# A hybrid attention block on one core: the variance of x enters the norms ahead of the power, three more warming products, the last gate's second part later, the last scaling behind the last squares

## The chip, the core and the metric

The kernel runs on one core of one Trainium2 chip. A core has five engines that work side by side: TensorE (PE, matrix products), VectorE (DVE), ScalarE (ACT), GpSimd (POOL) and SyncE (SP, which here only starts transfers). Transfers between the chip's memory (HBM) and the core's SBUF run on 16 DMA engines. The metric is the device time of one execution in microseconds (us); lower is better.

## The reference

One transformer block on x of 512 tokens by 1024 features, all in float32. Cut to what matters:

```python
n = rmsnorm(h, g_mix)
(gq, gk, gv, gr, z_gf, z_gb, cq, ckv, kr, z_ma, z_mb) = split(n @ w_in)
y_gla = gla_branch(...)      # 4 heads: gated linear attention, both directions, chunks of 64
    # o = rmsnorm(o_f + o_b, g_gla) per head (256 wide); o * silu(gr)
y_mla = mla_branch(...)      # 8 heads: softmax attention
    # q = rmsnorm(cq, g_q) @ w_uq, kv = rmsnorm(ckv, g_kv) @ w_ukv, rope on 32 columns
h = h + (sigmoid(z_ma) * y_gla + sigmoid(z_mb) * y_mla) @ w_out
m = rmsnorm(h, g_mlp)
h = h + square(relu(m @ w_ff1)) @ w_ff2      # 4096 hidden
return rmsnorm(h, g_final)

def rmsnorm(x, g): return x * rsqrt(mean(x * x) + EPS) * g
```

## The kernel before

Features or tokens lie on the 128 partitions; a tile is mostly 128 x 512. Every float32 product is split into a high and a low part and done as three products in the format fp32r (high by high, low by high, high by low), so each operand has tiles with names ending in h and l. The large products (gv, gr, za, w_out and the MLP) use seven block products in place of eight.

The names that matter here:

- `x` is not normalised before it is projected. The products run on x times `g_mix` (tiles `xT`), and the norm's factor r_x = 1/sqrt(var + EPS), one value for each token, is multiplied in later. Each later norm of something that came from x must therefore allow for r_x. For the heads' norm, `gla_squares` (L1140) lets ACT square the output `gla<h>o`, DVE forms mean + EPS in the tile `gla<h>ss` (128 x 4), POOL raises it to the power −0.5 (`mhalf` is −0.5), and DVE multiplies by `r_x`. `gla_gated` (L1150) then multiplies it into the gates `gra`, `grb`, `grc`, `grd` (tiles of `g1`), and `gla_turn` (L1157) turns those on PE (tiles `y`). For the ranks `cq` and `ckv` of the second branch, `rstd_diag` (L618) does the same: mean times r_x squared (`r_x2`), plus EPS, the power on POOL, times `r_x`.
- The head of the program (L663 on) starts with 8 products of a tile of ones (`warm`), which nothing reads, and goes on with the first projections (`first`), whose weights `vw` and input `x` come by DMA. The input is scaled by a column of `gvec`, which is a transfer of its own.
- `zb0` to `zb7` are the eight feature tiles of the gate z_mb; `gated` scales and squashes each. For the last one (L1626 to L1629) three of the eight blocks of the sum over features run first (`range(3)`), `rotary_q` comes between, and then the other five (`range(3, KD)`).
- `up_units(0)` brings up the first pair of softmax heads (tiles `uq`, `uk`, `uv`, weights `wq0`, `wk0`; `wq1` belongs to the next pair). `lin.out()` is the output of the last linear head, `gla3o`, from scores `sc` and states `st`. `s` are the softmax scores.
- The final norm works by blocks of 128 tokens: squares of the two halves with a running sum (`out_squares`, `out_square`, ACT), mean (DVE) and power (POOL) in `hp`, then the left half is scaled on DVE (`out_left`, tiles `sy`, `sz`) and the right half on ACT (`out_right`, tiles `row`), and each half is stored.

What sets the order: from `nc.keep()` on, after the head, each operation is only recorded as a `Work`, and `nc.flush` lets the class `Due` put all of them in order. `Due` gives each operation a due time, counted back from the PE product that needs it, and then plays the program through with the durations of `Work.cost`. At each step an engine takes, among the operations that are ready, the one that is due first. DVE and POOL share one port in this model, and where both could begin, an operation that `yields` gives way. The engines then follow that order. So an altered cost, or an operation more or less, can move any operation behind the head. All operations are issued from one line of `lay` (L229), which is why every row of the profile has that line: the rows are told apart by their tiles' names.

Of the kernel before, what the change touches and what calls it, by code (L numbers as in the profile page):

```python
# [15 lines left out]
ALU = mybir.AluOpType  # L16
# [125 lines left out]
class Work:  # L142
    def __init__(self, engine, name, args, named):
        self.engine, self.name, self.args, self.named = engine, name, args, named
        self.is_dma = name == "dma_start"
# [12 lines left out]
        self.yields = name in ("tensor_copy", "tensor_scalar")  # L158
        self.func = args[2] if name == "activation" else None

    def cost(self):
# [8 lines left out]
        if self.engine == "scalar":  # L170
            table = self.func not in (None, AF.Copy, AF.Identity, AF.Square)
            more = (0.03 if table else 0) + (0.1 if "accum_out" in self.named and n > 256 else 0)
            return more + (0.217 + 0.000543 * n if self.from_psum else 0.09 + 0.000857 * n)
        if self.engine == "vector":
            if "scan" in self.name:
                return 0.32
            if self.name == "copy_predicated":
                return 0.2
            if self.name == "scalar_tensor_tensor":
                return 0.125 + 0.00105 * n if not self.psum else 0.17 + 0.00085 * n  # L180
            return 0.065 + (0.00105 if two or self.psum or self.name == "tensor_reduce" else 0.00066) * n
# [16 lines left out]
class Script:  # L198
# [19 lines left out]
    def told(self, work):  # L218
        if self.kept is not None:
            self.kept.append(work)  # L220
            return None
        return self.lay(work)
# [23 lines left out]
class Due:  # L246


    def __init__(self, todo, slots, head=0.0, tables=None):
# [16 lines left out]
        for i, w in enumerate(todo):  # L266
# [26 lines left out]
            after[i].discard(i)  # L293

# [92 lines left out]
def tile_block(ctx: ExitStack, tc: tile.TileContext, t, out: bass.AP):  # L387
# [216 lines left out]
    r_x, r_x2 = one([P, NT], F32, "r_x"), one([P, NT], F32, "r_x2")  # L604
# [59 lines left out]
    for _ in range(8):  # L664
        nc.tensor.matmul(warm[:, :P], ones, ones, start=True, stop=True)
# [44 lines left out]
    nc.vector.tensor_tensor(r_x2, r_x, r_x, op=ALU.mult)  # L710
# [429 lines left out]
    def gla_squares(h, os):  # L1140
# [488 lines left out]
    gated(proj_run(zb, xT, None, range(3, KD)), "b7")  # L1629
# [4 lines left out]
    for _ in units:  # L1634
        pass
    rs = gla_squares(h, os)
# [113 lines left out]
    def out_square(i, cols):  # L1750
        p = hparts[i]
        nc.scalar.activation(out_at[i][0][:, cols], hrow[i][:, cols], AF.Square, accum_out=p[:, 1:2])
# [17 lines left out]
    def out_right(i):  # L1770
        right, rs = out_at[i][1], hparts[i][:, 3:4]
        nc.scalar.activation(right, right, AF.Copy, scale=rs)
# [101 lines left out]
    class Plan:  # L1874
        def add(self, engine, cost, fn, reads=(), writes=(), lands=None):
            if fn:
                fn()
# [5 lines left out]
    def act(size, fn, reads, writes):  # L1883
        plan.add("ACT", COST["ACT"][size], fn, reads, writes)
# [291 lines left out]
    class Group:  # L2176


        def __init__(self, qd):
            self.qd, self.last = qd, qd == NQ - 1  # L2180
            self.corner, self.right, self.out_key = {}, {}, {}
# [128 lines left out]
        def last_half(self, x, bank):  # L2310
# [15 lines left out]
            act(QUART, lambda: out_square(3, cols), (("row", 3, 0, "h"),), (("hp", 3), self.out_key[3][0]))  # L2326
# [3 lines left out]
        def ended(self, i, squared=False):  # L2330
# [6 lines left out]
            act(HALFT, lambda: out_right(i), (hp, right), (right,))  # L2337
# [121 lines left out]
```

## Time and profile before

| | |
|---|---|
| time, median of 3 runs | 744.87 us (744.81 to 746.26) |
| time of the profiled execution | 744.94 us |
| its span, from first to last record | 743.2 us |
| granted TensorE clock, mean over the span | 0.997 |
| HBM read, written | 116.81 MB, 2.10 MB |
| POOL busy | 193.9 us (26%) |

The span leaves out what lies around the records. A row of the profile names the line, the engine, the operation, and the tiles as output<-inputs, with shapes as partitions x elements; "x4" counts instructions. In a timeline the first number is the start in us and the second the duration, and brackets at the end give the idle time before and the instruction that ended it. Matmuls are pipelined, so the duration of one row reaches into the next; the pace is read from start to start. A small product of plain float32 shows as two records. The clock of a window is given as a share of full speed.

### The profile page before, as it was taken

To read this page: it belongs to the slowest core of one execution; us is meant where nothing else is said; L and a number is where in the kernel's file an instruction comes from. 1 tells how busy PE (TensorE), PEld (TensorE's weight loads), DVE (VectorE), ACT (ScalarE), POOL (GpSimd) and SP (SyncE) were. 2 spreads that over 40 slices of the span, in tenths; PEclk is the share of its full clock that TensorE was granted. 3 is DMA by queue.
4 is the path that set the end of the run, shared out by engine and by line. 5 is a ranking of instruction groups with operands and counts; after the bars stand their busy time and mean duration, and the time that the engine had idled before them with its cause. 6 is when DMAs were issued, how large, how long until landed. Compare 5 with 4: busy or idle time off the path is not lost.

```text
span 743.2 us, 11562 instructions
## 1 busy us (share of the span) xinstructions
PE 731.5 (98%) x4232; PEld 643.5 (87%) x4232; DVE 611.3 (82%) x960; ACT 511.5 (69%) x855; POOL 193.9 (26%) x203
## 2 busy tenths in 40 slices
PE   8999999999999999999999999999999999999996
PEld 6888888888889888899988899889988998889985
DVE  6595776759999879998989799867896798778885
ACT  7575665669989576889955778646864497348754
POOL 1123031301111214137753102322122201312433
PEclk9999999999999999999999999999999999999999
DMA  9959896652311314329966449999889997988993
GB/s 311 320 142 168 200 213 113 114 114 56 86 39 48 61 53 110 75 78 268 237 199 106 121 112 222 218 217 220 204 181 214 210 207 179 216 218 190 199 170 114
DMA packets 103930, 121.24 MB, mean 163 GB/s; under 512 B 16080, under 2 KB 67296, under 8 KB 103872
## 3 DMA queue, kind: packets, MB, share of 16 engines
q0 software_dynamic: 30384, 48.52, 39.0%
q1 hardware_dynamic: 73200, 71.45, 31.6%
q8 instruction: 33, 0.54, 0.3%
q10 hardware_dynamic: 288, 0.52, 0.2%
q14 instruction: 25, 0.20, 0.1%
HBM read 116.81 MB, written 2.10 MB: 160 GB/s over the span
## 4 chain that ended last, share of the span: by engine, by line
PE 94%; ACT 2%; DVE 2%; issue 1%; POOL 1%; DMA 1%; POOLq 0%; ACTq 0%; DVEq 0%
PE mb L229 23%; PE ab L229 16%; PE zb L229 4%; PE av L229 3%; PE first L229 3%; PE s L229 3%; PE wox L229 3%; PE gvx L229 3%; PE zax L229 3%; PE grx L229 3%; PE f L229 3%; PE cq L229 2%; PE gq L229 2%; PE tp L229 2%; PE gvz L229 1%; PE ckv L229 1%
## 5 line engine op out<-in xcount | busy, mean ns | idle before, releaser
L229 POOL DMA_DIRECT2D ms<-in_w_ff x37 | 46.5, 1331 | 116.5 <-DVE hl0l L229 35.9
L229 POOL DMA_DIRECT2D w1s<-in_w_ff x18 | 22.9, 1273 | 92.2 <-DVE hl0l L229 27.3
L229 DVE TENSOR_TENSOR h<-h,ab 128x512 f32<-128x512 f32 x48 | 31.7, 681 | 6.4 <-PE ab L229 6.4
L229 ACT ACTIVATE row<-row 128x512 f32<-128x512 f32 x49 | 30.6, 625 | 0.8
L229 PE MATMUL s<-kbuf,q 96*128 96x512 f32 x96 | 28.7, 410 | 0.1
L229 PE MATMUL av<-pT,v 128*128 128x256 f32 x192 | 27.9, 289 | 0.0
L229 PEld LDWEIGHTS av<-pT,v 128*128 128x128 f32 x192 | 24.9, 190 | 0.6
L229 ACT ACTIVATE e<-s,top 128x512 f32<-128x512 f32 x32 | 21.9, 686 | 3.7 <-DVE top L229 3.4
L229 DVE TENSOR_REDUCE top<-s 128x1 f32<-128x512 f32 x32 | 21.5, 682 | 2.4 <-PE s L229 2.1
L229 PE MATMUL mb<-four,hl0h 128*128 128x256 f32 x128 | 23.4, 283 | 0.0
L229 ACT ACTIVATE row<-mb 128x512 f32<-128x512 f32 x28 | 16.4, 584 | 10.0 <-PE mb L229 10.0
L229 DVE TENSOR_TENSOR pT<-tp,pT 128x512 fp32r<-128x512 f32 x32 | 21.4, 682 | 0.8 <-ACT pT L229 0.7
L229 DVE TENSOR_TENSOR hl1l<-ms,hl1h 128x1024 fp32r<-128x1024 f32 x12 | 14.7, 1223 | 8.2 <-ACT hl1h L229 8.1
L229 ACT ACTIVATE hl3h<-ms 128x1024 fp32r<-128x1024 f32 x13 | 13.8, 1059 | 11.1 <-PE ab L229 4.6
L229 PEld LDWEIGHTS mb<-four,hl0h 128*128 128x128 f32 x128 | 20.1, 192 | 0.5 <-ACT hl2h L229 0.3
L229 PE MATMUL mb<-four,hl3h 128*128 128x256 f32 x112 | 20.4, 283 | 0.0
L229 PE MATMUL mb<-m,hl2h 128*128 128x256 f32 x112 | 20.4, 283 | 0.0
L229 PE MATMUL mb<-four,hl2h 128*128 128x256 f32 x112 | 20.4, 283 | 0.0
L229 ACT ACTIVATE pT<-tp 128x512 fp32r<-128x512 f32 x32 | 19.0, 596 | 1.7 <-PE tp L229 1.5
L229 DVE TENSOR_TENSOR hl3l<-ms,hl3h 128x1024 fp32r<-128x1024 f32 x13 | 15.9, 1223 | 4.9 <-ACT hl3h L229 4.7
L229 ACT ACTIVATE hl1h<-ms 128x1024 fp32r<-128x1024 f32 x12 | 12.7, 1058 | 10.2 <-PE ab L229 3.1
L229 PE MATMUL tp<-ident,e 128*128 128x128 f32 x128 | 19.3, 273 | 0.0
(1146 smaller groups left out, 2814.1 us busy)
## 6 DMA issues: line engine op xcount, KB each, us to landing
ms<-in_w_ff POOLq DMA_DIRECT2D x37, 512.0 KB, 8.0
w1s<-in_w_ff POOLq DMA_DIRECT2D x18, 512.0 KB, 7.2
ms<-in_w_ff SPq DMA_DIRECT2D x16, 512.0 KB, 5.0
w1s<-in_w_ff SPq DMA_DIRECT2D x15, 512.0 KB, 5.8
w<-in_w_out POOLq DMA_DIRECT2D x10, 512.0 KB, 8.6
wf0f<-in_w_ff SPq DMA_DIRECT2D x10, 512.0 KB, 5.9
wf1f<-in_w_ff SPq DMA_DIRECT2D x10, 512.0 KB, 6.0
wf2f<-in_w_ff SPq DMA_DIRECT2D x10, 512.0 KB, 5.9
```

What stands on the lines that cost most here:

```text
L229: return call(*map(real, work.args), **{k: real(v) for k, v in work.named.items()})
```

## The change

Five things change.

1. **The variance ahead of the power.** `r_x2` goes. `x_var` = var + EPS of x and `x_eps` = EPS times `x_var` are kept. The heads' norm becomes (mean · x_var + x_eps) to the power −0.5, with no DVE multiplication behind the power; two DVE operations stand ahead of it, where there was one. For `cq` and `ckv` one DVE operation and the power remain, where there were three and the power.
2. **Three more warming products:** 11 in place of 8.
3. **The last gate's second part** (`zb7`, the last five blocks and `gated`) is recorded behind the first softmax heads and the last linear head's output.
4. **The last scaling behind the last squares.** An operation can now name others that it must follow (`behind`); the scaling of the right half of row block 2 follows the last squares of row block 3.
5. **The planner's costs.** ACT operations with a column as scale cost 0.08 more, those on fewer than 128 partitions 0.1 more; DVE operations on fewer than 128 partitions 0.08 more; the power gives way at the port.

```diff
@@ class Work
+        self.behind = []
-        self.yields = name in ("tensor_copy", "tensor_scalar")
+        self.yields = name in ("tensor_copy", "tensor_scalar") or named.get("op") == ALU.pow
+        self.part = 0 < len(outs) and outs[0].parts[1] - outs[0].parts[0] < 128
@@ cost
         if self.engine == "scalar":
             table = self.func not in (None, AF.Copy, AF.Identity, AF.Square)
             more = (0.03 if table else 0) + (0.1 if "accum_out" in self.named and n > 256 else 0)
+            more += 0.08 * isinstance(self.named.get("scale"), View) + 0.1 * self.part
...
             if self.name == "scalar_tensor_tensor":
-                return 0.125 + 0.00105 * n if not self.psum else 0.17 + 0.00085 * n
-            return 0.065 + (0.00105 if two or self.psum or self.name == "tensor_reduce" else 0.00066) * n
+                return 0.08 * self.part + (0.125 + 0.00105 * n if not self.psum else 0.17 + 0.00085 * n)
+            return 0.08 * self.part + 0.065 + (0.00105 if two or self.psum or self.name == "tensor_reduce" else 0.00066) * n
@@ class Due
+        at = {id(w): i for i, w in enumerate(todo)}
+        for i, w in enumerate(todo):
+            after[i].update(at[id(x)] for x in w.behind)
@@ rstd_diag
-        r = r_x if name == "x" else sm(f"{name}r")
+        r = sm(f"{name}r") if scaled else x_var
         if scaled:
-            nc.vector.scalar_tensor_tensor(r, tot[:, 0:NT], 1.0 / n, r_x2, op0=ALU.mult, op1=ALU.mult)
-            nc.vector.tensor_scalar(r, r, EPS, None, op0=ALU.add)
+            nc.vector.scalar_tensor_tensor(r, tot[:, 0:NT], 1.0 / n, x_eps, op0=ALU.mult, op1=ALU.add)
         else:
-            nc.vector.tensor_scalar(r, tot[:, 0:NT], 1.0 / n, EPS, op0=ALU.mult, op1=ALU.add)
-        nc.gpsimd.tensor_tensor(r, r, mhalf.to_broadcast([P, NT]), op=ALU.pow)
+            nc.vector.tensor_scalar(x_var, tot[:, 0:NT], 1.0 / n, EPS, op0=ALU.mult, op1=ALU.add)
+        to = r if scaled else r_x
+        nc.gpsimd.tensor_tensor(to, r, mhalf.to_broadcast([P, NT]), op=ALU.pow)
+        r = to
...
-        if scaled:
-            nc.vector.tensor_tensor(r, r, r_x, op=ALU.mult)
@@ the head
-    for _ in range(8):
+    for _ in range(11):
         nc.tensor.matmul(warm[:, :P], ones, ones, start=True, stop=True)
...
-    nc.vector.tensor_tensor(r_x2, r_x, r_x, op=ALU.mult)
+    nc.vector.tensor_scalar(x_eps, x_var, EPS, None, op0=ALU.mult)
@@ gla_squares
-        nc.vector.tensor_scalar(tot, tot, 1.0 / GDV, EPS, op0=ALU.mult, op1=ALU.add)
+        nc.vector.scalar_tensor_tensor(tot, tot, 1.0 / GDV, x_var, op0=ALU.mult, op1=ALU.mult)
+        nc.vector.tensor_tensor(tot, tot, x_eps, op=ALU.add)
         nc.gpsimd.tensor_tensor(tot, tot, mhalf.to_broadcast([P, NT]), op=ALU.pow)
-        nc.vector.tensor_tensor(tot, tot, r_x, op=ALU.mult)
@@ the last linear head
     ro = rotary_q()
-    gated(proj_run(zb, xT, None, range(3, KD)), "b7")
     units = up_units(0)
...
     for _ in units:
         pass
+    gated(proj_run(zb, xT, None, range(3, KD)), "b7")
     rs = gla_squares(h, os)
@@ last_half
-            act(QUART, lambda: out_square(3, cols), (("row", 3, 0, "h"),), (("hp", 3), self.out_key[3][0]))
+            square = act(QUART, lambda: out_square(3, cols), (("row", 3, 0, "h"),), (("hp", 3), self.out_key[3][0]))
+            self.scaled[2].behind.append(square)
@@ ended
-            act(HALFT, lambda: out_right(i), (hp, right), (right,))
+            self.scaled[i] = act(HALFT, lambda: out_right(i), (hp, right), (right,))
```

The order changes nearly everywhere behind the head. Three places are shown. A row gives the line, the operation, and output<-inputs with running numbers; `TENSOR_SCALAR` stands for the forms with a column or a constant, and the line of `lay` is 232 in the changed file.

DVE at the norm of linear head 0, before (`qkb`, `qkf` are scaled queries of the next head, `mb` a gate's bias):

```order
L229 TENSOR_SCALAR gla0ss_1779<-gla0ss_1779 128x4
L229 TENSOR_TENSOR qkb_1788<-gqn_265_1405,eeb_1769 128x512
L229 TENSOR_TENSOR qkf_1776<-gqn_265_1405,eef_1760 128x512
L229 TENSOR_TENSOR gla0ss_1779<-gla0ss_1779,r_x 128x4
L229 TENSOR_SCALAR mb_1848<-gateb_1806,gvec 128x512
L229 TENSOR_SCALAR gra_515<-gla0o_333_1742,gla0ss_1779,gra_515 128x256
```

and changed (`r_x_81` is `x_var`, `r_x_82` is `x_eps`; `c3b`, `c3f` are decay factors, `ckv0l` the low part of a weight):

```order
L232 TENSOR_SCALAR gla0ss_1783<-gla0ss_1783,r_x_81 128x4
L232 TENSOR_TENSOR qkb_1792<-gqn_265_1409,eeb_1773 128x512
L232 TENSOR_TENSOR gla0ss_1783<-gla0ss_1783,r_x_82 128x4
L232 TENSOR_TENSOR qkf_1780<-gqn_265_1409,eef_1764 128x512
L232 TENSOR_SCALAR mb_1846<-gateb_1810,gvec 128x512
L232 TENSOR_TENSOR c3b_1852<-e3b_1761 128x1
L232 TENSOR_TENSOR c3f_1854<-e3f_1740 128x1 x2
L232 TENSOR_TENSOR c3b_1852<-e3b_1761 128x1
L232 TENSOR_TENSOR ckv0l_1859<-ckv0f_1644,ckv0h_1746 128x1024
L232 TENSOR_SCALAR gra_519<-gla0o_333_1744,gla0ss_1783,gra_519 128x256
```

Both small operations now stand ahead of the power, the second behind `qkb`; between it and the gate there are four one-column products and `ckv0l` more.

DVE at the norm of linear head 2, before (`ang` and `turns` belong to the rotary tables, `diff`, `difb` to the decay of the next head):

```order
L229 TENSOR_SCALAR gla2ss_2307<-gla2ss_2307 128x4
L229 TENSOR_TENSOR difb_2355<-rrb_2118 128x512
L229 COPY ang_2370<-pos_i_492 128x512
L229 TENSOR_TENSOR gla2ss_2307<-gla2ss_2307,r_x 128x4
L229 TENSOR_TENSOR qkf_2376<-gkn_413_2168,eef_2357 128x512
L229 TENSOR_SCALAR grb_686<-gla2o_450_2278,gla2ss_2307,grb_686 128x256
```

and changed:

```order
L232 TENSOR_SCALAR gla2ss_2320<-gla2ss_2320,r_x_81 128x4
L232 TENSOR_SCALAR ang_2370<-ang_2370,gvec 128x512
L232 TENSOR_TENSOR gla2ss_2320<-gla2ss_2320,r_x_82 128x4
L232 TENSOR_TENSOR qkb_2381<-gkn_413_2166,eeb_2368 128x512
L232 TENSOR_SCALAR turns_2387<-ang_2370 128x512
L232 TENSOR_TENSOR qkf_2362<-gqn_384_2041,eef_2346 128x512
L232 TENSOR_TENSOR qkb_2381<-gqn_384_2041,eeb_2368 128x512
L232 TENSOR_SCALAR turns_2387<-turns_2387 128x512
L232 TENSOR_TENSOR c3f_2408<-e3f_2336 128x1 x2
L232 TENSOR_SCALAR ang_2370<-turns_2387,ang_2370 128x512
L232 TENSOR_SCALAR grb_690<-gla2o_450_2291,gla2ss_2320,grb_690 128x256
```

Between the last small operation of the norm and the gate stand eight operations, where there was one. On PE the turning of this head (`y`) moves behind six more `cq` products.

PE at the last gate, before (the end of `zb7` and what follows):

```order
L229 MATMUL zb_544_2713<-xT_8_89,zb7l_2480 128x512
L229 MATMUL zb_544_2713<-xT_9_90,zb7h_2453 128x512 x2
L229 MATMUL zb_544_2713<-xT_9_90,zb7l_2480 128x512
L229 MATMUL uq_568_2811<-cqhl_533_2726,wq0h_2622 128x512 x2
L229 MATMUL uq_568_2811<-cqhl_533_2726,wq0l_2634 128x512
```

and changed:

```order
L232 MATMUL uv_573_2903<-wk0h_2758,ckvhl_502_2604 128x256
L232 MATMUL zb_544_2709<-xT_5_87,zb7h_2476 128x512
L232 MATMUL zb_544_2709<-xT_5_87,zb7l_2502 128x512
L232 MATMUL zb_544_2709<-xT_6_88,zb7h_2476 128x512 x2
L232 MATMUL zb_544_2709<-xT_6_88,zb7l_2502 128x512
```

The second part of `zb7` moves behind `uk`, `gla3o` and `uv` of the first softmax heads; `uq` of the next pair (`wq1`) follows it.

On ACT's last rows the scaling of row block 2 changes places with the second square of row block 3.

More of the change, by code (lines that the diff above doesn't have):

```diff
@@ L220, in told @@
             self.kept.append(work)
-            return None
+            return work
         return self.lay(work)
@@ L601, in proj_T @@
         return proj_run(proj_begin(w_in, col, name, tag), xT)
-    r_x, r_x2 = one([P, NT], F32, "r_x"), one([P, NT], F32, "r_x2")
+    r_x, x_var, x_eps = (one([P, NT], F32, f"r_x{i}") for i in range(3))
     R = u2("R")
@@ L1751, in out_square @@
         p = hparts[i]
-        nc.scalar.activation(out_at[i][0][:, cols], hrow[i][:, cols], AF.Square, accum_out=p[:, 1:2])
+        return nc.scalar.activation(out_at[i][0][:, cols], hrow[i][:, cols], AF.Square, accum_out=p[:, 1:2])
     def out_partial(i):
@@ L1771, in out_right @@
         right, rs = out_at[i][1], hparts[i][:, 3:4]
-        nc.scalar.activation(right, right, AF.Copy, scale=rs)
+        return nc.scalar.activation(right, right, AF.Copy, scale=rs)
     def out_store(i, x):
@@ L1875, in add @@
         def add(self, engine, cost, fn, reads=(), writes=(), lands=None):
-            if fn:
-                fn()
+            return fn() if fn else None
     plan = Plan()
@@ L1883, in act @@
     def act(size, fn, reads, writes):
-        plan.add("ACT", COST["ACT"][size], fn, reads, writes)
+        return plan.add("ACT", COST["ACT"][size], fn, reads, writes)
     def dve(size, fn, reads, writes):
@@ L2180, in __init__ @@
             self.qd, self.last = qd, qd == NQ - 1
-            self.corner, self.right, self.out_key = {}, {}, {}
+            self.corner, self.right, self.out_key, self.scaled = {}, {}, {}, {}
         def rows(self, x, g):
```

## The prediction

> **What bounds the kernel now.** I read four views: the page's busy times and chain, the waits of TensorE (PE), the table of windows with the granted clock, and timelines at the places where the change acts. First the page:
>
> ```profile
> PE 731.5 (98%) x4232; PEld 643.5 (87%) x4232; DVE 611.3 (82%) x960; ACT 511.5 (69%) x855; POOL 193.9 (26%) x203
> PE 94%; ACT 2%; DVE 2%; issue 1%; POOL 1%; DMA 1%; POOLq 0%; ACTq 0%; DVEq 0%
> ```
>
> PE is busy 731.5 of 743.2 us and has 94% of the chain that ended last. So only three things can move the end: PE's own work, its idle 11.7 us, and the clock it is granted. The change removes no PE product outside the warm-up, so it comes down to the idle time and the clock. PE's waits, longest first (engine and tile, what released it, total us, times, longest):
>
> ```profile
> PE first L229 <- ACT xT L229: 1.8, 1, 1.8
> PE warm L229 <- DVE ones L229: 1.1, 1, 1.1
> PE y L229 <- DVE gra L229: 0.9, 1, 0.9
> PE uq L229 <- DVE gla3ss L229: 0.3, 1, 0.3
> ```
>
> The first is the gap between the warming products and the first real ones. Here is PE's head (start, duration, instruction, count, idle before), then PE's busy time, instructions, clock, DMA share and GB/s by window:
>
> ```profile
> 1.11 3.69 PE L229 MATMUL warm<-ones 128*128 128x128 f32 x16 [1.11 <-DVE ones L229]
> 6.58 1.20 PE L229 MATMUL first<-xT,first0h 128*128 128x512 f32 x4 [1.77 <-ACT xT L229]
> 7.97 2.07 PE L229 MATMUL first<-xT,first0l 128*128 128x512 f32 x4 [0.19 <-DVE first0l L229]
> 9.84 2.72 PE L229 MATMUL first<-xT,first0h 128*128 128x512 f32 x8
> 12.39 1.07 PE L229 MATMUL first<-xT,first0l 128*128 128x512 f32 x4
> 13.30 1.07 PE L229 MATMUL first<-xT,first0h 128*128 128x512 f32 x4
> 4.59:8.00 3.41, 1.45 (x7) 1.00 1.04 372
> 8.00:11.41 3.41, 3.41 (x8) 0.50 1.05 398
> 11.41:14.82 3.41, 3.41 (x16) 1.00 1.09 360
> 735.03:738.45 3.42, 1.66 (x14) 1.00 0.45 169
> 738.45:741.86 3.41, 0.00 (x0) 1.00 0.78 292
> 741.86:743.20 1.34, 0.00 (x0) 0.50 0.00 0
> ```
>
> The clock changes only at 8.00, 11.41 and 741.86, which lie on one grid of 3.41 us. The window 4.59 to 8.00, in which PE worked 1.45 of 3.41 us (42%), is followed by one at 0.50. The window 735.03 to 738.45, with 1.66 of 3.42 (49%), is followed by one at 1.00, and the empty one behind it by 0.50. So a window seems to set the clock of the next, with a limit between 42% and 49%. The price shows in the head: four products take 13.30 − 12.39 = 0.91 us at full clock; the twelve between 7.97 and 12.39 take 4.42 where 3 × 0.91 = 2.72 would do, a loss of 1.70 us (3.41 × 0.5 = 1.71 by the clock).
>
> **Part 1, three more warming products.** The 8 products are 16 records in 3.69 us, 0.23 us each, so three more are 6 records: 1.38 us at that pace, half of it if the full clock of 4.59 serves them. The warm-up then ends between 4.80 + 0.69 = 5.49 and 6.18, still ahead of the 6.58 at which xT lets PE go on. The products cost nothing, since they fill the gap of 1.77 us; without that cover they'd cost up to 1.38. The window 4.59 to 8.00 then holds 1.45 + 0.69 = 2.14 to 2.83 us of work (63 to 83%), above the 49% that kept the clock. I therefore expect 1.00 in 8.00 to 11.41, and the loss of **1.7 us** gone: bounds 0 (the clock falls all the same) and −1.71.
>
> [...]
>
> Can PE use the faster clock, with operands 1.7 us earlier? In the head its last operand, and later the closest split, are:
>
> ```profile
> 8.49 0.69 DVE L229 TENSOR_TENSOR first0l<-vw,first0h 128x512 fp32r<-128x512 f32 x1
> 40.36 1.22 DVE L229 TENSOR_TENSOR gr10l<-grw,gr10h 128x1024 fp32r<-128x1024 f32 x1
> 43.12 0.39 PE L229 MATMUL grx<-gr10l,xT 128*128 128x512 f32 x1
> ```
>
> The split of the second weight ends at 9.18; its products start at 12.39, or 10.69 at the new pace. gr10l is ready at 41.58 for a product at 43.12, which would come at 41.42. That is 0.16 us late at most, so little of the 1.7 is given back.
>
> **Part 2, the variance ahead of the power.** It bears on PE at head 0 of the gated linear attention, where PE waits 0.9 us (DVE, POOL and DVE rows, and last a row of the chain):
>
> ```profile
> 200.58 0.16 DVE L229 TENSOR_SCALAR gla0ss<-gla0ss 128x4 f32<-128x4 f32 x1
> 201.25 0.68 DVE L229 TENSOR_TENSOR qkf<-gqn,eef 128x512 f32<-128x512 f32 x1
> 200.82 2.02 POOL L229 TENSOR_TENSOR gla0ss<-gla0ss,mhalf 128x4 f32<-128x4 f32 x1 [16.57 <-DVE gla0ss L229]
> 202.82 1.01 POOL L229 TENSOR_TENSOR qsb<-qkb,qsb 128x384 fp32r<-128x384 f32 x1
> 202.87 0.98 DVE L229 TENSOR_TENSOR gla0ss<-gla0ss,r_x 128x4 f32<-128x4 f32 x1 [0.94 <-POOL gla0ss L229]
> 203.77 0.74 DVE L229 TENSOR_SCALAR mb<-gateb,gvec 128x512 f32<-128x512 f32 x1
> 204.43 0.86 DVE L229 SCALAR_TENSOR_TENSOR gra<-gla0o,gla0ss,gra 128x256 f32<-128x256 f32 x2
> 205.75 0.94 PE y L229 x6
> ```
>
> The 4-element product behind the power took 0.98 us, while POOL's qsb ran (202.82 to 203.83), and mb and gra stood behind it. It goes; one stands ahead of the power instead, in front of qkf, and before gra DVE now has mb, four c3 products of one column and ckv0l, a split of 1024 elements (1.22 for gr10l's split of that shape, above). So qkf starts at 201.33 to 201.41 (a tiny operation takes 0.08 to the next start by head 2's rows below, 0.16 by its length), mb 0.60 to 0.68 later, c3 0.66 to 0.74 after that, ckv0l after 0.32 to 0.64, and gra 1.2 after it: 204.1 to 204.7 against 204.43. The power starts at 201.4 and, even at the old 2.02 us, is done at 203.4, ahead of that. Ends: −0.9 (the whole wait goes) and +0.3. I take **−0.4**, by the pitch from start to start, which is how DVE's rows in this stretch follow each other. The ckv and cq norms lose two tiny DVE operations each; PE shows no wait there, so 0.
>
> What is late next? Head 2, where the planner put more between the norm and the gates. Before:
>
> ```profile
> 243.81 0.16 DVE L229 TENSOR_TENSOR gla2ss<-gla2ss,r_x 128x4 f32<-128x4 f32 x1 [0.56 <-POOL gla2ss L229]
> 243.89 0.68 DVE L229 TENSOR_TENSOR qkf<-gkn,eef 128x512 f32<-128x512 f32 x1
> 244.49 0.87 DVE L229 SCALAR_TENSOR_TENSOR grb<-gla2o,gla2ss,grb 128x256 f32<-128x256 f32 x2
> 246.10 0.38 PE L229 MATMUL y<-ident,grb 128*128 128x128 f32 x2
> ```
>
> grb was ready at 245.36, PE came 0.74 later. Now three 512-wide qk products (0.68 each), two one-tensor turns and ang (mb's 0.74 each at most), and two c3 stand there instead of one qk product: up to 2.9 us more, and PE gets six cq products (0.23 each, 1.4 in all) ahead of its turning. New wait: 0 to 2.9 − 1.4 − 0.74 = 0.8.
>
> **Part 3, zb7 later.** Fourteen products of 0.23 (3.2 us) leave their place ahead of uq<-wq0h and go behind uv, right before uq<-wq1h:
>
> ```profile
> 295.96 0.28 PE L229 MATMUL uv<-wk0h,ckvhl 128*128 128x256 f32 x1
> 296.52 0.70 PE L229 MATMUL uq<-cqhl,wq1h 128*128 128x512 f32 x2 [0.28 <-DVE gla3ss L229]
> 297.29 0.61 PE L229 MATMUL uq<-cqhl,wq1h 128*128 128x512 f32 x2
> 298.05 2.29 PE L229 MATMUL s<-kbuf,q 96*128 96x512 f32 x9
> ```
>
> PE idles 0.28 before uq, 0.07 inside it and 0.15 before the scores; the moved products cover the first and give DVE 3.2 us for the rest: **−0.3**, ends 0 and −0.5. Against it, uq, uk and gla3o come 3.2 us earlier, and DVE must have the states and the rotary work by then. With the heads' gates behind more work, I put all new waits of the reordered middle together at **+0.4**, half of head 2's bound; ends 0 and +1.3 (0.8 there, 0.5 here if zb7's cover turns into an equal wait).
>
> **Part 4, the last scaling behind the last square.** ACT's last rows:
>
> ```profile
> 737.07 0.74 DVE L229 SCALAR_TENSOR_TENSOR sy<-h,hp,w1s 128x512 f32<-128x512 f32 x1
> 737.34 0.40 ACT L229 ACTIVATE sz<-h 128x256 f32<-128x256 f32 x1
> 738.10 0.55 POOL L229 TENSOR_TENSOR hp<-hp,mhalf 128x1 f32<-128x1 f32 x1 [1.43 <-DVE hp L229]
> ```
>
> The last square, sz, stood behind the scaling of row block 2 and ended at 737.74; now that scaling follows it. But DVE's sy, row block 2's left half, ends at 737.81, and the mean that feeds the last power (738.10) stands behind it on DVE: 0.16 for such an operation and some 0.1 for the hand-over would let the power start at 738.0. So **−0.1**, ends −0.1 and +0.2 (row block 2's right half is stored later, among the last stores).
>
> **Part 5, the planner's costs** add no instruction; they are the reason that nearly all of the middle moves, and their price is in the terms above.
>
> **Sum.** −1.7 − 0.4 − 0.3 + 0.4 − 0.1 = −2.1. The profiled execution took 744.94, the span 743.2 and 1.7 around it, and the median is 744.87, the same within 0.07. So **742.8 us**.
>
> **Rivals.** (1) *The clock falls all the same*, because what counts isn't the busy share of that window. For it: the rule rests on one window on each side of the limit. Against it: the change of clock lies on the grid, right behind the window with PE's longest gap. Then −2.1 + 1.7 = −0.4: 744.5. (2) *The middle gives it back*: no wait of head 0 or zb7 goes, head 2 waits its 0.8, the last head half as much; −1.7 − 0.1 + 0.8 + 0.4 = −0.6: 744.3. For it: DVE is 82% busy and its order is changed throughout; against it, the planner set the old order by the same rules, and the waits quoted are the longest that it left. (3) *Slower: DVE becomes the bound in the heads.* In the old order each head had about 0.74 us between gate and turning (head 2's). Where the gates come 2.9 later and no cq products cover them, PE waits 2.9 − 0.74 = 2.2 per head; from the second such head on this beats the 2.5 gained elsewhere (the sum without its +0.4): −2.5 + 4.4 = +1.9, or 746.8. Against it: in the quoted case PE did get the cq products. That transfers hide the gain I give no case: no DMA stands in the waits quoted.
>
> **How the numbers follow.** Forecast 0.62, rival 1 0.20, rival 2 0.12, rival 3 0.06. The forecast's own range is 741.6 (the whole of head 0's wait, zb7's 0.5, no new wait: −1.7 − 0.9 − 0.5 − 0.1 = −3.2, and 0.1 of the small waits left out above) to 743.7 (+1.3 of new waits in place of +0.4). The 8-in-10 range reaches over rivals 1 and 2 and, below, a little past the best sum for waits that the planner may clear elsewhere: 741.2 to 744.9. About what a measurement can tell from no change is 0.2%, 1.5 us, so faster means below 743.4. That holds in some nine tenths of the forecast's chance and in an eighth of rivals 1 and 2: 0.60. Slower is rival 3 and a little: 0.07. The same: 0.33.
>
> **What would show it.** Part 1: the clock in the second half of the first 12 us is 1.00 and the twelve products after the first four take 2.7 us. Part 2: y waits for gra under 0.6 us; grb may newly appear among PE's waits. Part 3: uq's wait for gla3ss is gone. Part 4: the last rows end 0.1 earlier after PE's last product. The prediction is wrong if the clock still shows 0.50 there, or if PE's list shows over 1.5 us of waits that weren't in the old one.

## The result, and the profile after

The changed kernel takes 741.95 us (median of 5 runs, 741.32 to 742.66), the kernel before 744.81 (744.14 to 746.26). The ratio is 0.996 (95% interval 0.9945 to 0.9974). It is faster by 2.9 us or 0.4%, 0.8 more than the 2.1 forecast. The profiled execution took 742.11 with a span of 740.4, so the two profiled executions differ by 2.83 and their spans by 2.8. The accounts below are made between these.

The page of the changed kernel:

```profile
PE 730.2 (99%) x4238; PEld 643.3 (87%) x4238; DVE 606.2 (82%) x956; ACT 512.2 (69%) x855; POOL 193.6 (26%) x203
PE 87%; DVE 5%; DMA 3%; ACT 2%; issue 1%; POOL 1%; POOLq 0%; DVEq 0%; ACTq 0%
```

PE's idle time went from 11.7 to 10.2 us, and its busy time fell by 1.3 although three products were added: the window 8.00 to 11.41 of the kernel before, at clock 0.50, counts as busy in all its 3.41 us, so a clock kept up shows in PE's busy time. DMA's share of the chain goes from 1% to 3% (2% of it a weight of the MLP). PE's waits:

```profile
PE s L232 <- DMA q<-ro: 1.4, 1, 1.4
PE warm L232 <- DVE ones L232: 1.1, 1, 1.1
PE first L232 <- ACT xT L232: 0.4, 1, 0.4
PE ab L232 <- DVE h L232: 0.4, 1, 0.4
PE first L232 <- DVE first0l L232: 0.2, 1, 0.2
```

The waits of `y` for `gra` (0.9) and of `uq` for `gla3ss` (0.3) are gone, and a new one of 1.4 us stands where the softmax scores `s` wait for transfers. One of 0.4 us, of `ab` for `h` in the MLP, is new too; the kernel without part 4, whose order is the same up to the tail, doesn't show it.

**The head.** PE's rows, and the windows (PE busy, instructions, clock, DMA share, GB/s):

```profile
1.11 4.84 PE L232 MATMUL warm<-ones 128*128 128x128 f32 x22 [1.11 <-DVE ones L232]
6.31 1.21 PE L232 MATMUL first<-xT,first0h 128*128 128x512 f32 x4 [0.36 <-ACT xT L232]
7.69 1.20 PE L232 MATMUL first<-xT,first0l 128*128 128x512 f32 x4 [0.17 <-DVE first0l L232]
8.73 1.99 PE L232 MATMUL first<-xT,first0h 128*128 128x512 f32 x8
```

```profile
5.58:8.99 3.41, 2.88 (x13) 1.00 1.03 374
8.99:12.40 3.41, 3.41 (x17) 1.00 1.05 396
```

The grid of 3.41 us lies elsewhere than before, where 4.59 and 8.00 were on it. Here the trace's first clock entry, full speed, is at 5.58, and the warming products, 0.21 us apart until then, end with one that follows in 0.13. The window behind it holds 84% of work, the next keeps 1.00. The first products start at 6.31, not 6.58, since the first transfers landed sooner in this execution: ACT, which waits for `gvec` there, begins `xT` at 5.53 and not at 5.80.

**Two landmarks** split the rest: `xss` (sums of x's squares, the end of the head) and `ckvss` (sums for `ckv`, behind linear heads 0 to 2). The same products lie between them in every kernel here. Groups by tile, before and then changed (after the count: shortest, median and longest in ns; then the first and last start):

```profile
L229 PE MATMUL xss<-ones,sq x8: 164/250/250, 25.1 to 25.8; 128*128 128x1 f32 x8
L229 PE MATMUL ckvss<-ones,ckvs x8: 164/250/250, 252.4 to 253.1; 128*128 128x1 f32 x8
```

```profile
L232 PE MATMUL xss<-ones,sq x8: 164/250/250, 23.2 to 23.9; 128*128 128x1 f32 x8
L232 PE MATMUL ckvss<-ones,ckvs x8: 164/250/250, 249.4 to 250.1; 128*128 128x1 f32 x8
```

To two decimals the first ones start at 25.09 and 252.43 before, at 23.25 and 249.37 now. From the first product to `xss`: 25.09 − 6.58 = 18.5 before, 23.25 − 6.31 = 16.9 now, so 1.6 us of clock; 0.3 more is the earlier start, which no part of the change brought. From `xss` to `ckvss`: 227.3 before, 226.1 now, so 1.2 us in the linear heads. The last PE product starts at 736.41 before and 733.55 now, 2.86 earlier; `ckvss` was 3.06 earlier, so what follows it lost 0.2. From the last product to the end of the span it is 6.8 in both.

**The scores.** SP's queue and PE in the changed kernel, then SP's queue before:

```profile
288.48 1.87 SPq L232 DMA_DIRECT2D kbuf<-kbuf  x3
290.45 6.25 SPq L232 DMA_DIRECT2D q<-ro  x10
295.36 1.86 PE L232 MATMUL s<-kbuf,q 96*128 96x512 f32 x7 [1.36 <-DMA q<-ro]
```

```profile
292.45 7.57 SPq L229 DMA_DIRECT2D q<-ro  x12
300.12 1.17 SPq L229 DMA_DIRECT2D kbuf<-kbuf  x2
```

The rotated parts of the queries go into the tiles `q` by small transfers, about 0.63 us apart on SP. Now the three copies of the rotary key stand ahead of them (1.87 us). The transfer that completes the first head's `q` lands 0.13 us before `s` starts; it lands 0.09 before `s` in the kernel before too (297.96 and 298.05). So this queue held the scores in both.

### The profile page after: what moved, and what is told of

Its sections match the earlier page's. It is cut to its first block, busy times and chain, and to the rows that moved or that the text cites. A ratio compares the mean times of both kernels' runs of the same rounds, so it can differ in the third digit from the quotient of the medians.

```text
span 740.4 us, 11575 instructions
## 1 busy us (share of the span) xinstructions
PE 730.2 (99%) x4238; PEld 643.3 (87%) x4238; DVE 606.2 (82%) x956; ACT 512.2 (69%) x855; POOL 193.6 (26%) x203
## 4 chain that ended last, share of the span: by engine, by line
PE 87%; DVE 5%; DMA 3%; ACT 2%; issue 1%; POOL 1%; POOLq 0%; DVEq 0%; ACTq 0%
PE mb L232 21%; PE ab L232 14%; PE zb L232 4%; PE f L232 3%; PE av L232 3%; PE wox L232 3%; PE gvx L232 3%; PE zax L232 3%; PE grx L232 3%; PE first L232 3%; PE s L232 2%; DMA ms<-in_w_ff 2%; PE cq L232 2%; PE tp L232 2%; PE gvz L232 1%; PE ckv L232 1%
## 5 line engine op out<-in xcount | busy, mean ns | idle before, releaser
L232 PE MATMUL mb<-four,hl0h 128*128 128x256 f32 x128 | 23.4, 283 | 0.0
L232 ACT ACTIVATE hl3h<-ms 128x1024 fp32r<-128x1024 f32 x13 | 13.8, 1058 | 10.5 <-PE ab L232 4.6
```

The lines of the kernel that those rows point to most:

```text
L232: return call(*map(real, work.args), **{k: real(v) for k, v in work.named.items()})
```

## The experiments

Times are medians; the kernel before had 744.7 to 744.8 in each set. In the tables, "head" is from the first product to `xss` and "heads" is from `xss` to `ckvss`.

| kernel | time | ratio to before (95%) | head | heads |
|---|---|---|---|---|
| before | 744.8 | | 18.5 | 227.3 |
| changed | 741.95 | 0.996 (0.9945 to 0.9974) | 16.9 | 226.1 |
| before, 11 warming products | 743.34 | 0.9981 (0.9972 to 0.9989) | 16.9 | 227.4 |
| changed, 8 warming products | 742.78 | 0.997 (0.9959 to 0.9982) | 18.5 | 226.6 |
| before, new norm | 746.89 | 1.0036 (1.0019 to 1.0052) | 16.9 | 227.5 |
| before, new costs | 750.29 | 1.0078 (1.0058 to 1.0097) | 16.9 | 229.1 |
| before, new norm and costs | 745.93 | 1.0014 (1.0006 to 1.0023) | 19.1 | 226.1 |
| changed, old costs | 744.62 | 1.0002 (0.9994 to 1.0011) | 16.9 | 227.4 |
| changed, old norm | 745.60 | 1.0023 (1.0012 to 1.0035) | 16.9 | 229.1 |
| changed, zb7 early | 744.50 | 0.9999 (0.999 to 1.0008) | 16.9 | 226.1 |
| changed, key copies late | 741.75 | 0.9967 (0.9955 to 0.9979) | 16.9 | 226.1 |
| the same, first head's q first | 742.65 | 0.9974 (0.9963 to 0.9985) | 16.9 | 226.1 |
| changed, scaling free | 742.54 | 0.9966 (0.9953 to 0.9979) | 17.0 | 227.1 |
| before, warm-up split | 744.73 | 0.9999 (0.999 to 1.0008) | 18.4 | 227.4 |

### The warm-up

On the kernel before:

```diff
-    for _ in range(8):
+    for _ in range(11):
         nc.tensor.matmul(warm[:, :P], ones, ones, start=True, stop=True)
```

> The kernel before with 11 warming products and nothing else. Theory (the busy share of a 3.41 us window sets the clock of the next one): granted clock 1.00 in the window behind the head's first, the twelve products there take 2.7 us, the sums of x (xss) start 1.6 us earlier than the old 25.23, and the time falls by 1.6 to about 743.2; PE's waits for gra and gla3ss stay as they were. Rival (the changed kernel's head was earlier because its first transfers happened to land 0.27 us sooner): at most 0.3 less, about 744.5, and the clock falls to 0.50 again.

Measured: 743.34, 1.5 less. `xss` comes at 23.6, 1.5 sooner, though the first product started later than before (6.67). The windows:

```profile
4.77:8.18 3.41, 2.12 (x12) 1.00 1.01 374
8.18:11.59 3.41, 3.41 (x16) 1.00 1.05 394
```

PE still waited 1.1 us for `xT`, and at 62% the clock stayed. The rival falls: the transfers weren't sooner, and the gain was there. The other way round, 8 products in the changed kernel:

> The changed kernel with 8 warming products in place of 11. Theory: clock 0.50 for one window in the head, twelve products in 4.4 us, time 1.6 above the changed kernel's, about 743.5; the wait of the scores s for the transfers q stays at 1.4. Rival: no difference to the changed kernel beyond 0.3 (742.0), clock 1.00.

In the profiled execution, its slowest, the head took 18.5 again, and the wait for `q` was 1.4. But the median is only 0.8 above the changed kernel's (742.78, 741.2 to 744.69), half of what was expected; the heads of all profiles, below, show why. The next experiment deals the eight products otherwise, on the kernel before:

```diff
-    for _ in range(8):
+    for _ in range(7):
         nc.tensor.matmul(warm[:, :P], ones, ones, start=True, stop=True)
+    nc.tensor.matmul(warm[:, :P], ones, xraw[1][:, 0:P], start=True, stop=True)
```

> The kernel before with its eight warming products dealt otherwise: seven at once, the eighth on the second tile of x, which lands near 5.5 us and so in the middle of PE's gap. The busy time of the window 4.59 to 8.00 stays near 1.45 of 3.41 us (43%), the longest gap falls from 1.8 to about 1.2 us. Theory (the busy share sets the clock of the next window): 0.50 again behind it, time as before, 744.8 within 0.4. Rival (a long gap is what drops the clock): 1.00 there, time about 743.3.

The time is the one that the theory named, but the experiment doesn't decide between theory and rival. Here is its head, then a window of it, and the same window of the kernel with the key copies late (11 products, shown further down):

```profile
1.11 3.35 PE L229 MATMUL warm<-ones 128*128 128x128 f32 x14 [1.11 <-DVE ones L229]
5.56 0.80 PE L229 MATMUL warm<-x,ones 128*128 128x128 f32 x2 [1.10 <-DMA x<-in_xt]
6.51 2.07 PE L229 MATMUL first<-xT,first0h 128*128 128x512 f32 x4 [0.15 <-ACT xT L229]
8.38 1.91 PE L229 MATMUL first<-xT,first0l 128*128 128x512 f32 x4
10.09 2.26 PE L229 MATMUL first<-xT,first0h 128*128 128x512 f32 x8
```

```profile
3.77:7.18 3.41, 2.16 (x8) 1.00 1.02 372
3.80:7.22 3.42, 3.08 (x14) 1.00 1.05 381
```

The products run at half pace (four take 8.38 − 6.51 = 1.87, then 1.71) up to about 10.5, with no halving at 8.00. The column of the granted clock shows 1.00 all the same: the trace's first clock entry, full speed, is at 10.60, and where there is no entry the column reads 1.00. It does so over the warming products of every profile, which run 0.21 us apart until the first entry and about 0.11 apart behind it (the warm-up alone, at 4.77). So ahead of the first entry it is the pace that has to be read, and here no product was at full pace before 10.60: nothing was halved, the clock had not come up yet.

Over all profiled heads the pattern is plain. With 11 products eight of eight took 16.9 to 17.0. With 8 products four of six took 18.4 to 19.1 and two (new norm, new costs) 16.9. There are two ways to lose. In the kernel before and in the changed one with 8 products, full speed came early (4.58, 5.26), and a thin window behind it (42%, 50%) took it away for the next. With the split warm-up and with norm and costs it came only at 10.60 and 12.49. In all fourteen heads the first step to full speed stands right behind the first window that PE filled to 81% or more; windows of 79% and less, at half pace, didn't bring it. The two rows above are such a pair, on almost the same grid: with 63% the clock didn't come up behind the window, with 90%, the warming work being longer, it did. So in these heads the loss is there in some executions and not in others, as the grid lies, and three more products take both kinds away in all that were seen. The times agree: 11 runs of the warm-up alone lie within 0.7 us, 28 of the kernel before in the same set within 2.8.

Is it the length of the gap or the busy share of the window that drops the clock? Traces of the other kernels tell more than the split warm-up. Below are a window and the next one from the changed kernel with 8 products (the head), the kernel before with the new costs, and the changed one with zb7 early, and then three windows in a row from the one with the first head's q first:

```profile
5.26:8.67 3.41, 1.70 (x6) 1.00 1.03 380
8.67:12.08 3.41, 3.41 (x10) 0.50 1.05 390
360.20:363.61 3.41, 1.85 (x12) 1.00 0.93 164
363.61:367.02 3.41, 3.41 (x16) 0.50 1.07 228
356.07:359.48 3.41, 1.85 (x13) 1.00 0.92 178
359.48:362.89 3.41, 3.41 (x26) 1.00 1.06 220
298.66:302.07 3.41, 2.67 (x20) 1.00 0.61 115
302.07:305.48 3.41, 2.25 (x15) 1.00 0.50 108
305.48:308.89 3.41, 3.41 (x26) 1.00 0.00 0
```

The length of the gap alone doesn't decide: a wait of 1.90 us that the grid splits over two windows (78% and 66% busy) left the clock at full, and one of 1.92 within one window (44%, in the kernel with the new norm, below) halved it. In these traces the busy share decides outside a band: every window under 48% was followed by half speed, none over 55% was. Inside it both came: 50% and 54% were followed by 0.50, 49% (the end of the kernel before) and 54% by 1.00. The two windows of 54% have the same wait of 1.56 us, so what decides there is open.

### The norm and the costs

The norm alone (part 1) on the kernel before, with the edits of `rstd_diag`, `x_eps` and `gla_squares` as in the diff above:

> The kernel before with the variance ahead of the power (part 1) and nothing else; DVE's order at head 0 is then the same as in the changed kernel. Theory (removing the small product behind the power and the order that follows from it takes the whole wait of head 0): PE's wait of y for gra is gone, and the time falls by 1.2 to about 743.6. Rival (the gain of head 0 came mostly from the planner's costs): y still waits 0.5 or more, and the time falls by 0.4 at most, to 744.4. Either way the clock falls to 0.50 in the head and the scores wait as before (under 0.4).

The costs alone (part 5: `part`, the two cost terms, `yields` for the power):

> The kernel before with the planner's new costs and nothing else (part 5 alone); the norm is the old one, with its product by r_x behind the power, now put behind ckv0l. Theory (part 5 gives the heads' gain): y's waits for gra fall from 1.5 together to 0.4 or less, xss to ckvss takes 226.2 to 226.5 in place of 227.4, time about 743.9; the clock in the head is 0.50 as before. Rival (the norm is needed for it): the waits stay over 1.0 and the time is 744.5 to 745.

The changed kernel without part 5, and without part 1:

> The changed kernel with the planner's old costs and the power not yielding (without part 5). DVE's order at head 0 from the norm to the gates is the same as in the changed kernel. Theory (the heads' 1.2 us came from DVE being brought forward by 1 us ahead of the norm, which the new costs did): y waits for gra 0.7 or more in heads 0 and 1 together, the stretch from xss to ckvss takes 227.2 in place of 226.1, and the time is 1.0 above the changed kernel's, about 743.0. Rival (it came from the norm): the stretch stays at 226.1 to 226.4, time 742.

> The changed kernel with the old norm (without part 1). DVE's order at head 0 then has the product by r_x between ckv0l and the gate. Theory (under the new costs it is the missing product that keeps DVE clear of POOL): one-column and four-column DVE operations there take near 1 us beside POOL's qsb and qsf again, y waits for gra 1.5 us or more in head 0 and as much in head 1, and the time is 3 above the changed kernel's, about 745. Rival (parts 1 and 5 add up without a bond): y waits under 0.8 in all, time 742.5.

And both on the kernel before:

> The kernel before with parts 1 and 5 and nothing else. Theory (the two together give the heads' gain): xss to ckvss takes 226.1 to 226.4, y waits for gra 0.3 or less, and the time is that of the kernel without the zb7 move plus the loss of the clock, 744.5 to 746. Rival (the heads' gain needs the zb7 move or the warm-up too): the stretch takes 227 or more.

The stretch `xss` to `ckvss` can be read as a table of two by two: neither part 227.3, the norm alone 227.5 (227.4 in the changed kernel without the costs), the costs alone 229.1 (the same in the changed kernel without the norm), both 226.1. Neither part gains anything alone, the costs alone lose 1.8, and together they gain 1.2. With the norm alone `y` still waits 0.9 for `gra`, 0.6 and 0.3 in two heads, as the rival had it. With the costs alone, PE's wait, and DVE's rows at head 0, are:

```profile
PE y L231 <- DVE gra L231: 3.1, 2, 1.6
```

```profile
200.07 0.99 DVE L231 TENSOR_TENSOR c3b<-e3b 128x1 f32<-128x1 f32 x1
200.98 1.21 DVE L231 TENSOR_TENSOR ckv0l<-ckv0f,ckv0h 128x1024 fp32r<-128x1024 f32 x1
202.11 0.95 DVE L231 TENSOR_TENSOR gla0ss<-gla0ss,r_x 128x4 f32<-128x4 f32 x1
203.10 0.88 DVE L231 SCALAR_TENSOR_TENSOR gra<-gla0o,gla0ss,gra 128x256 f32<-128x256 f32 x2
```

A product of one column takes 0.99 and one of four columns 0.95, beside POOL's `qsb` (200.02 to 201.04) and `qsf` (201.00 to 203.04); the others of their kind in this stretch take 0.15. The planner counts a DVE operation at the port only above 99 elements a partition (`Work.shares`), so it doesn't see this. The same place in the changed kernel, where the product is gone:

```profile
197.73 0.15 DVE L232 SCALAR_TENSOR_TENSOR gla0ss<-gla0ss,r_x 128x4 f32<-128x4 f32 x1
198.41 0.15 DVE L232 TENSOR_TENSOR gla0ss<-gla0ss,r_x 128x4 f32<-128x4 f32 x1
200.10 1.22 DVE L232 TENSOR_TENSOR ckv0l<-ckv0f,ckv0h 128x1024 fp32r<-128x1024 f32 x1
201.23 0.87 DVE L232 SCALAR_TENSOR_TENSOR gra<-gla0o,gla0ss,gra 128x256 f32<-128x256 f32 x2
```

And with the norm under the old costs, DVE's order here is the same, but it reaches the norm 198.94 − 23.4 = 175.5 us behind `xss`, and in the changed kernel 197.73 − 23.2 = 174.5: the costs bring DVE forward by 1.0 us ahead of the norm. That is the share which the norm's own rows don't show. Which of the cost changes does it wasn't tried.

The totals hold more than the heads. Without the costs the changed kernel is 2.7 slower, where 1.0 was expected; the profiled executions differ by 2.4, 1.3 of it here and 0.8 behind `ckvss`, where `s` waits 1.7 (1.4 in the changed kernel) and `tp` 0.3. With the costs alone neither theory nor rival had the loss of 5.5: behind `ckvss` the profile has waits of 1.3 (`uq`), 0.6 and 1.6 (`s`), and the halved window at 363.61 shown above. With the norm and the costs on the kernel before, the time is 1.2 above before: the head was at half pace for longer (19.1), and `s` waited 1.6 at 361. The norm alone was expected to gain 1.2 and lost 2.1, although the head of its profiled execution lost nothing. Its profile shows where (PE's row at the scores, then windows):

```profile
298.52 2.00 PE L229 MATMUL s<-kbuf,q 96*128 96x512 f32 x5 [1.92 <-issue]
```

```profile
295.63:299.04 3.41, 1.49 (x7) 1.00 0.69 102
299.04:302.45 3.41, 3.41 (x10) 0.50 0.79 163
```

The transfers `q<-ro` took 4 us and more to land in this execution (4.17 for the first head's last one, 2.3 in the kernel before), the scores waited 1.9, PE was busy 44% of that window, and the next ran at half clock. A wait of 1.9 us thus cost about 1.9 + 1.7 = 3.6.

### The last gate

The changed kernel with `gated(..., "b7")` put back behind `rotary_q()`:

> The changed kernel with the second part of zb7 at its old place. SP's queue then has the transfers q<-ro ahead of the copies of the rotary key (kbuf<-kbuf) again. Theory (the move brought the 1.4 us wait of s and took away about 1.4 us of old waits, so it is worth nothing): the wait for q is under 0.4, the old waits of ro, uq and s are back with 1.2 to 1.4 together, and the time is that of the changed kernel within 0.3 (742.0). Rival (the move was a plain loss): no old wait comes back, time 740.6. Second rival (the move was a gain): time 743 or more.

At the place itself the theory nearly held: `uq` waits 0.8 and `s` 0.3 there, in place of 1.4 for `q`; `ro` doesn't wait. But the median is 2.5 us above the changed kernel's, which is the second rival's time, and the profiled execution, its fastest, 0.9. The rest comes 60 us later (DVE, then PE):

```profile
353.87 3.44 DVE L232 TENSOR_TENSOR bo20l<-bo20f,bo20h 128x1024 fp32r<-128x1024 f32 x1
358.77 1.43 PE L232 MATMUL s<-kbuf,q 96*128 96x512 f32 x5 [1.56 <-ACT e L232]
```

This split takes 1.20 in the changed kernel, where it was put at 348.3. At 353.87 it falls beside four POOL products and a transfer's issue (353.14 to 358.12) and takes 3.44; the row maxima and the exponentials queue behind it, and the scores wait 1.56. Other orders meet it too: norm and costs on the kernel before (3.43), the new costs alone (3.47) and the changed kernel with the old norm (3.86, and a wait of 2.4). The window of this wait is the one of 54% above that kept the clock; with the costs alone its like lost it. Of the eleven runs with zb7 early, the five with a mean clock of 0.995 average 745.0 and the other six 743.9, so a halved window is likely to come on top in some; no profile of such a run was taken. So what the zb7 move is worth lies in the order that the planner made from it, and not in the waits that it covers.

Then the key copies, which the move had put ahead of the queries on SP (changed kernel; `behind` is the change's own means):

```diff
+                key_copies.append(nc.sync.dma_start(raw(kb[r]), raw(res[0][r])))
...
+                if pr == 0:
+                    for late in key_copies:
+                        late.behind.append(copy)
```

> The changed kernel with the three copies of the rotary key (kbuf<-kbuf) held behind the first pair's four transfers q<-ro on SP's queue. Theory (the scores start when the fifth q transfer has landed, and the 1.87 us of key copies ahead of it are the wait): the first q<-ro is issued near 289.1 in place of 290.45, the wait of s for q falls from 1.4 to 0.2 or less, and the time falls by 1.2 against the changed kernel, to about 740.8. Rival (something else, DVE's states or keys, holds the scores as well): the wait only changes its name, s starts within 0.4 us of where it did, and the time stays at 741.8 to 742.

`s` started at 294.35, 1.0 sooner, 0.09 behind the landing of the first head's last transfer, which is what the theory said of the cause. The wait stayed:

```profile
294.35 2.32 PE L232 MATMUL s<-kbuf,q 96*128 96x512 f32 x9 [1.52 <-ACT wk2h L232]
```

The planner, which holds such a transfer for cheap (0.06 us in `Work.cost`, against the 0.63 here), now put `uq` behind the scores, and so took away what had filled the time. The median gained 0.2, which can't be told from nothing. One step further, with the other transfers behind the first head's two:

```diff
+                if pr or i:
+                    copy.behind.extend(first_copies)
+                else:
+                    first_copies.append(copy)
```

> The kernel with the key copies late, and besides with all other transfers q<-ro behind the two of the first head, so that the first head's second transfer is the second on SP and not the fifth. Theory (that transfer's landing is what starts the scores): it is issued about 1.8 us earlier, lands near 292.4, and s follows the last product of zb7 with no wait over 0.3; the time falls by 1.3 to 1.5 against the kernel with the key copies late, to about 740.3. Rival (the wait comes out elsewhere): s starts early, but uq, tp or av of the next products wait as long, and the time stays at 741.5 or more.

```profile
292.75 2.23 PE L232 MATMUL s<-kbuf,q 96*128 96x512 f32 x9
303.23 0.94 PE L232 MATMUL s<-kbuf,q 96*128 96x512 f32 x3 [1.90 <-DMA kbuf<-kbuf]
```

The scores now start with no wait at 292.75, and the second head's wait 1.9 for a key copy instead. The rival held: the queue of some fifteen small transfers is what is short, and putting one first makes another last. No version here beats the changed kernel by more than its runs differ. Dealing the transfers over two queues wasn't tried.

### The last scaling

The changed kernel without `self.scaled[2].behind.append(square)`:

> The changed kernel without part 4, the last scaling of row block 2 ahead of the second last square again. Theory (part 4 moves the last power by under 0.1 and the last stores take it back): from the start of the last product to the last power 1.7 in place of 1.6 us, from there to the end 0.1 less, time as the changed kernel within 0.5 (741.5 to 742.5). Rival (the scaling did hold the end): 0.4 or more longer from the last product to the end.

From the last product to the last power it is 736.18 − 734.50 = 1.68 us, in the changed kernel 735.17 − 733.55 = 1.62, and from there to the end 5.1 and 5.2. Part 4 is worth nothing. But this kernel, whose order differs from the changed one's in the tail alone, showed waits of `y` for `gra` of 1.1 us. Its rows at head 0:

```profile
200.63 2.05 DVE L232 TENSOR_TENSOR ckv0l<-ckv0f,ckv0h 128x1024 fp32r<-128x1024 f32 x1
```

```profile
200.59 1.01 POOL L232 TENSOR_TENSOR qsb<-qkb,qsb 128x384 fp32r<-128x384 f32 x1
```

and POOL's row in the changed kernel:

```profile
200.05 2.16 POOL L232 TENSOR_TENSOR qsb<-qkb,qsb 128x384 fp32r<-128x384 f32 x1
```

`qsb` and `ckv0l` start within 0.05 us of each other in both, and one of them takes over 2 us in place of 1.0 to 1.2: POOL's in the changed kernel's profile (2.16 against 1.01), DVE's here (2.05 against 1.22). It is the same in the second head (`cq0l` 2.06 here, 2.05 in the changed kernel with 8 products, 1.22 in the others). So of the heads' 1.2 us a part is there in some executions only: with both parts it is 226.1 where DVE goes first, 226.6 where it loses once, 227.1 where it loses twice.

## Why the prediction was right

**The clock** (−1.7): right in the place and the size. The head lost 1.6 us of half pace in the profile of before and none now; the warm-up alone gave 1.5 in the median. What the prediction didn't see is that the loss is not in every execution, and that a second kind, a clock that comes up late, goes with the first. Its rule held in a second place (44% busy in the window at 295.63 of the kernel with the new norm, and 0.50 behind it), but its limit between 42% and 49% is too sharp: windows of 50% and 54% were followed by 0.50 too. Rival 1's time is out. Its reason, that the busy share of the window isn't what counts, has the record against it outside 48 to 55%, and is open inside.

In all fourteen heads the pace is half up to a first step between 4.50 and 12.49. In four places waits of 1.6 to 1.9 us, with the window 42 to 54% busy, were followed by half clock.

**The norm** (−0.4, bounds −0.9 and +0.3): the right sign, but 1.2 was measured, beyond the bound, and the total is off by about as much as this term. The step that failed is the one that placed `gra` by adding the new rows to DVE's old times ("qkf starts at 201.33"), with the sentence on part 5 that its price is in the terms above. The costs had moved DVE 1.0 us forward ahead of that place, and the 0.9 of the list was not all that stood there either. The two parts need each other, which no row of before could show, and 1.0 of the 1.2 hangs on which of DVE and POOL gets its operation through first (226.1 to 227.1). The stretched DVE rows shown here, `c3b` (two columns of one tile, 0.99), the product by r_x (0.95), `ckv0l` (2.05) and `bo20l` (3.44), all have two inputs; whether that decides it wasn't tried.

**zb7** (−0.3) **and the new waits** (+0.4): together +0.1, and behind `ckvss` 0.2 was lost. The sum was right, the parts were not, so that it came out is luck. The old waits of `uq` (0.28 and 0.07) went as said, and one of `ro` (0.25) besides; the 0.15 ahead of the scores grew. The new one, 1.4 us, is neither at head 2 (no wait there) nor on DVE: it is on SP's queue, which the prediction didn't look at when it said that no DMA stands in the waits quoted. The scores stood behind the q transfers already, 0.09 us after the landing, and the list put that wait under another name.

**The last scaling** (−0.1, ends −0.1 and +0.2): 0.06 sooner at the last power, and from the last product to the end 6.8 as before: 0, within its two ends. Of the 2.83 between the two profiled executions, 0.3 belongs to no term: the first transfers landed sooner.

**Rival 3**, DVE as the bound of the heads, is real: with the costs and without the norm `y` waited 3.1 us in two heads, 1.6 and 1.5, against the 2.2 worked out, and the kernel was 0.8 us slower than before with the rest of the change and 5.5 without. The change as it stands keeps off it. Rival 2 would have given 744.3; what the middle gave back was one wait of 1.4, and the heads' gain paid for it.

## What to carry to other kernels

Judge a wait of PE by its window as well as by its length: here one that left a window of 3.41 us less than about half full (under 48% always, up to 54% at times) cost 1.7 us more in the next, and filling such a gap with three useless products paid 1.5. Where a planner orders everything, small edits can't be priced one by one: on the kernel before, the norm and the costs lost 2.1 and 5.5 us alone and 1.2 together, and yet taking either of them, or the zb7 move, out of the changed kernel lost 2.5 us or more. So a part is to be tried both ways, and its worth holds for that order alone. When work is moved past transfers, read each queue's rows around it: the small transfers on SP stood 0.63 us apart here, one behind the other, and the scores started 0.09 to 0.13 us behind the landing of the first head's last one.

## What was not expected of the hardware

- In all fourteen heads the first products ran at half pace, and the column of the granted clock doesn't show it: it reads 1.00 up to the first entry (at 10.60 in one head), over products 0.43 us apart in place of 0.23. With 63 to 79% of a window busy the clock didn't come up; with 81% and more it did.
- A DVE operation of one column took 0.99 us beside a POOL product, and a DVE split 3.44 in place of 1.20. Which of the two engines loses is not fixed: with starts 0.04 to 0.05 us apart, `qsb` took 2.16 and `ckv0l` 1.22 in one execution, 1.01 and 2.05 in another.
- Transfers of 16 rows (`q<-ro`), which landed after a median of 2.5 us before (2.3 to 2.9) and 2.4 in the changed kernel (2.2 to 3.3), took 4.2 to 4.9 in the one with the new norm, behind a 256 KB transfer that took 5.7 in place of the 3.8 of the kernel before.
